# A decoder layer on one core: feed-forward operand sums, hidden loads and the last column blocks in the mixers' pools

## The chip, the core and the metric

The kernel runs on one core of a Trainium2 chip. Times are device microseconds (us) of one execution. The time before is the median of three timed runs; beside it stands one execution taken by the hardware profiler, from which all rows come. PE is TensorE (PEld its weight loads), DVE VectorE, ACT ScalarE, POOL GpSimd, SP SyncE, which here only issues transfers.

## The reference

One layer with 512 tokens (SEQ), D_MODEL 2048 and D_FF 8192, all in float32:

```python
proj = x @ w_in[l]
...
mixed = jax.nn.sigmoid(ga) * y_a + jax.nn.sigmoid(gb) * y_b
x = layer_norm(ALPHA * x + mixed @ w_out[l], ln1_gain[l], ln1_bias[l])
h = jnp.square(jax.nn.relu(x @ w_ff1[l])) @ w_ff2[l]
x = layer_norm(ALPHA * x + h, ln2_gain[l], ln2_bias[l])
```

The change lies in the last two lines and in what joins them to the lines ahead: the two feed-forward products and the second layer norm.

## The kernel before

**Split products.** Every float32 operand is split in two: ACT copies it to a rounded high part, DVE subtracts that from the source for the low part (`split`, L85 and L86). A product is three matmuls, high by high, high by low, low by high (`mm3`, L115 to L117). A raw weight tile of 128 x 1024 thus costs a load of 512 KB, one ACT and one DVE operation, and feeds 24 matmuls of 512 columns, or 24 of 256.

**Up to the feed-forward.** The two mixers, the gated merge and the output projection run first. The output projection's last 256 columns go token tile by token tile: after each, `ln1(t)` normalizes the tile's 128 tokens, transposes them on PE (L646), splits them into the resident operand pair `bh`, `bl` (16 blocks of 128 features x 512 tokens each) and stores the tile to DRAM (`zd`) for the second residual.

**First product, the heads.** It has 32 groups of 256 hidden columns. The first four (NHEAD) are plain products of four raw weight tiles each (`head`); groups 0 and 1 are begun on the first half of the tokens. A group ends with Relu and Square on ACT (L715, L716) and a POOL transfer to DRAM (`keep`, `hd[g]`, L689). Raw tiles and their splits rotate through the mixers' pool `pw` (raw 3, high 3, low 2 buffers).

**First product, Strassen.** Groups 4 to 31 use seven products instead of eight on 256-token halves (`prod1`, q1 to q7). For these, DVE first forms sums of the halves of x from `bh` and `bl` (`whole` and `tt`, L744) and `put` splits them: q6, q7, q3 into tiles of their own, q5 back into the half of `bh`, `bl` that the heads have read. That happens twice (`u`), each time for four of the eight blocks. Weight sums (`b11`, `t2_`, `b12`) are made by DVE per group, results are put together by ACT and DVE (`E`, `U2`, `U3`, `R`), and each group's last two products run inside the next (`tail`, `left`).

**Where the pools change.** All pools of the mixers are closed by `mctx.close()` after the heads; the pools `fw` (raw 7, high 4, low 4) and `fx` of the Strassen part are opened on that memory. A tile in reused memory waits until the last reader of what lay there is done, and the `keep` transfers are such readers. The same happens after the Strassen part, where `fx` is closed and `fy` opened on its place for the hidden operand.

**Second product.** Four blocks of 512 columns (`cg`), each over 32 steps (`k2`) of 256 hidden features. A step loads h from `hd` (again for each block), loads a tile of `w2`, splits both and issues 24 matmuls into four PSUM banks, six for each token tile; the residual tiles come from `zd` on the ACT queue (`resid`, L837), all 16 of them as soon as their memory is free. `close` adds the residual and takes statistics. In the last block the last four steps (RES) are kept: their operands are split into `bh`, `bl`, and each token tile gets its last 24 matmuls, then `close`, layer norm and four output transfers (L894).

**What sets the order.** The program is written as above, and a scheduler then fixes each engine's order and the waits between engines; each engine takes its instructions strictly in that order, the issues of transfers on the ACT and POOL queues among them.

Of the kernel before, what the change touches and what calls it, by code (L numbers as in the profile page):

```python
# [36 lines left out]
RES = 8  # L37
# [15 lines left out]
def layer(ctx, tc, xt, xn, win, wa, wb, wo1, wo2, w1, w2, cst, vec, lnv, out):  # L53
# [533 lines left out]
    pf = mctx.enter_context(tc.tile_pool(name="pf", bufs=1))  # L587
# [95 lines left out]
    def load1(pool, g, b, bufs):  # L683
        raw = pool.tile([P, 1024], F32, tag="raw", bufs=bufs, name=nm("raw"))
        nc.sync.dma_start(out=raw[:], in_=w1[g, b])
        return raw[:]

# [13 lines left out]

    og = {}
# [6 lines left out]
    for g in range(NHEAD):  # L709
        if g not in og:  # L710
            og[g] = [ps("mm"), ps("mm")]
            head(g, og[g], None)
        r = pf.tile([P, 2, T], F32, tag="r", bufs=2, name=nm("r"))
# [25 lines left out]
    for q in ("q6", "q7", "q3"):  # L739
        t_ = fx.tile([P, 2, 8, CG], F32R, tag="x" + q, bufs=1, name=nm("x" + q))  # L740
        xo[q] = (t_[:, 0], t_[:, 1])

    def tt(dst, a, b, op):
        DVE.tensor_tensor(dst, a, b, op=op)  # L744

    for u in range(2):
        k = slice(4 * u, 4 * u + 4)

        def whole(q):
            pool, tag, bufs = (fw, "t2", 2) if q == "q4" else (fx, "st", 3)  # L750
            r = pool.tile([P, 4, CG], F32, tag=tag, bufs=bufs, name=nm("xr"))
            tt(r[:], xo[q][0][:, k, :].bitcast(F32), xo[q][1][:, k, :].bitcast(F32), ALU.add)
            return r

        def put(q, src):
            split(xo[q][0][:, k, :], xo[q][1][:, k, :], src[:])

        a11, a21 = whole("q1"), whole("q5")
        s3 = fw.tile([P, 4, CG], F32, tag="t2", bufs=2, name=nm("s3"))
        tt(s3[:], a11[:], a21[:], ALU.subtract)  # L760
        put("q7", s3)
        a22 = whole("q4")
        tt(a22[:], a21[:], a22[:], ALU.add)
        tt(a11[:], a22[:], a11[:], ALU.subtract)
        put("q6", a11)
        a12 = whole("q2")
        tt(a12[:], a12[:], a11[:], ALU.subtract)
        put("q3", a12)
        put("q5", a22)

    def tmp(tag, bufs):
        return fx.tile([P, CG], F32, tag=tag, bufs=bufs, name=nm(tag))[:]
# [20 lines left out]
    for g in range(NHEAD, NG):  # L793
        A, B, C = ps6(0), ps6(1), ps6(2)
        R = fx.tile([P, 2, T], F32, tag="st", bufs=3, name=nm("R"))
        E, U2, U3 = tmp("E", 2), tmp("U2", 2), tmp("U3", 1)
        b11 = load1(fw, g, 0, 7)
        prod1(A, "q1", b11, True, False)
        ACT.activation(E, A[:, :CG], AF.Copy)
        b12, b22 = load1(fw, g, 1, 7), load1(fw, g, 3, 7)  # L800
        tt(b11, b12, b11, ALU.subtract)
        t2_ = fw.tile([P, 1024], F32, tag="t2", bufs=2, name=nm("t2"))[:]
# [6 lines left out]
        b21 = load1(fw, g, 2, 7)  # L809
# [15 lines left out]
    def hload(k2):
        raw = fw.tile([P, 1024], F32, tag="raw", bufs=7, name=nm("hraw"))
        nc.sync.dma_start(out=raw[:], in_=hd[k2][:])
        return raw[:]

    def w2load(cg, k2):  # L830
        raw = fw.tile([P, 1024], F32, tag="raw", bufs=7, name=nm("raw"))
        nc.sync.dma_start(out=raw[:], in_=w2[cg, k2])
        return raw[:]

    def resid(t, cg):
        z = fy.tile([P, T], F32, tag=f"z{t}_{cg}", bufs=1, name=nm("z"))[:]
        nc.scalar.dma_start(out=z, in_=zd[t][:, cg * T:(cg + 1) * T])  # L837
        zt[t, cg] = z
# [6 lines left out]
    for cg in range(4):  # L845
        end = cg == 3
        o = [ps8() for _ in range(NT)]
        n2 = NG - (RES // 2 if end else 0)
        for k2 in range(n2):
            hh = fy.tile([P, 1024], F32R, tag="hh", bufs=3, name=nm("hh"))  # L850
            hl = fy.tile([P, 1024], F32R, tag="hl", bufs=3, name=nm("hl"))
            split(hh[:], hl[:], hload(k2))
            hh, hl = wview((hh, hl), T)
            wh, wl = wview(wsplit(w2load(cg, k2)), T)
            for k in range(2):
                for t in range(NT):
                    ts = slice(t * P, (t + 1) * P)
                    mm3(o[t][:], hh[:, k, ts], hl[:, k, ts], wh[:, k, :], wl[:, k, :],
                        k2 == 0 and k == 0, not end and k2 == NG - 1 and k == 1)
# [35 lines left out]
    wctx.close()  # L895
# [69 lines left out]
```

## Time and profile before

| | us |
|---|---|
| median of three runs (2744.82 to 2748.64) | 2748.24 |
| profiled execution | 2750.08 |
| its span from first to last instruction | 2748.3 |
| PE busy in it | 2673.1 |
| DVE busy | 1513.8 |
| ACT busy | 1124.3 |

The profiled execution lies 1.84 us over the median; 1.8 us of its time lie outside the span. The busy times say which engine leads. Where that engine stands still is read from its waits and from windows around them. In a window's row, "busy (x)" is the busy time and the number of instructions, and PEclk the granted clock as a share of full speed; two levels occur, 2.4 GHz (1.00) and 1.2 GHz (0.50), and a value between them is a stretch with both.

### The profile page before, as it was taken

What the parts mean: (1) busy time and instruction counts of PE and PEld (TensorE: products, weight loads), DVE (VectorE), ACT (ScalarE), POOL (GpSimd) and SP (SyncE); (2) the same over time, 40 slices, a digit from 0 to 9 for tenths busy, and PEclk for the clock granted to TensorE, in tenths of its full rate; (3) what the DMA queues carried; (4) which work ended last, traced back from release to release, by engine and by line L of the source; (5) the groups of instructions that cost most, each with busy time, mean ns of one, the idle gap of its engine ahead of it and who ended that gap; (6) DMA issues with size and microseconds to landing.
All of it is one profiled execution on the core that took longest, in us unless ns stands there. A gap on an engine that the chain in (4) does not pass through costs nothing. (4 is left out here: it accounts for less than half of the span.)

```text
span 2748.3 us, 37420 instructions
## 1 busy us (share of the span) xinstructions
PE 2673.1 (97%) x15264; PEld 2351.2 (86%) x15264; DVE 1513.8 (55%) x1985; ACT 1124.3 (41%) x1539; POOL 178.9 (7%) x152
## 2 busy tenths in 40 slices
PE   8999999999999999999978999999989999999997
PEld 8889788888888888889968999999978888888885
DVE  4588876564222222434738777777744444544546
ACT  4576646443222222322524454444543333333333
POOL 0110312210000000000200000000000000000001
PEclk9999999999999999999998999999999999999998
DMA  5322222222333333533533444434476566665663
GB/s 183 92 75 72 75 68 79 77 78 85 100 100 93 99 98 94 192 96 119 169 123 100 138 131 126 136 124 138 131 257 196 191 198 192 192 197 190 195 194 113
DMA packets 101549, 364.55 MB, mean 133 GB/s; under 512 B 11392, under 2 KB 12160, under 8 KB 99840
## 3 DMA queue, kind: packets, MB, share of 16 engines
q1 hardware_dynamic: 91584, 326.50, 38.4%
q0 software_dynamic: 5760, 25.17, 2.3%
q10 hardware_dynamic: 4032, 10.49, 1.0%
q8 instruction: 120, 1.97, 0.3%
q14 instruction: 53, 0.43, 0.0%
HBM read 336.94 MB, written 25.17 MB: 132 GB/s over the span
## 5 line engine op out<-in xcount | busy, mean ns | idle before, releaser
L86 DVE TENSOR_TENSOR wl<-raw,wh 128x1024 fp32r<-128x1024 f32 (+1 forms) x503 | 618.7, 1230 | 590.4 <-PE mm L117 335.8
L85 ACT ACTIVATE wh<-raw 128x1024 fp32r<-128x1024 f32 (+1 forms) x503 | 528.1, 1051 | 792.5 <-PE mm L116 585.6
L115 PE MATMUL mm<-bh,wh 128*128 128x512 f32 (+1 forms) x1920 | 665.8, 347 | 10.8 <-ACT wh L85 10.2
L117 PE MATMUL mm<-bh,wl 128*128 128x512 f32 (+1 forms) x1920 | 664.7, 347 | 2.9 <-DVE wl L86 2.9
L116 PE MATMUL mm<-bl,wh 128*128 128x512 f32 (+1 forms) x1920 | 665.9, 347 | 0.0
L115 PEld LDWEIGHTS mm<-bh,wh 128*128 128x128 f32 x1920 | 365.7, 191 | 54.6 <-ACT wh L85 10.9
L117 PEld LDWEIGHTS mm<-bh,wl 128*128 128x128 f32 x1920 | 365.2, 190 | 46.6 <-DVE wl L86 3.6
L116 PEld LDWEIGHTS mm<-bl,wh 128*128 128x128 f32 x1920 | 365.7, 190 | 42.7
L86 DVE TENSOR_TENSOR hl<-hraw,hh 128x1024 fp32r<-128x1024 f32 x124 | 151.7, 1225 | 358.5 <-ACT hh L85 358.5
L85 ACT ACTIVATE hh<-hraw 128x1024 fp32r<-128x1024 f32 x124 | 131.3, 1060 | 413.2 <-PE mm L116 392.6
L115 PE MATMUL mm<-wh,hh 128*128 128x512 f32 x496 | 193.5, 390 | 0.0
L117 PE MATMUL mm<-wh,hl 128*128 128x512 f32 x496 | 193.4, 390 | 0.0
L116 PE MATMUL mm<-wl,hh 128*128 128x512 f32 x496 | 193.4, 390 | 0.0
L115 PE MATMUL mm<-wh,bh 128*128 128x256 f32 (+1 forms) x448 | 139.3, 313 | 6.5 <-ACT bh L85 5.6
L115 PE MATMUL mm<-xq,wh 128*128 128x256 f32 x448 | 127.6, 285 | 16.3 <-ACT wh L85 16.3
L115 PE MATMUL tp<-wh,hh 128*128 128x512 f32 x368 | 143.4, 390 | 0.0
L117 PE MATMUL tp<-wh,hl 128*128 128x512 f32 x368 | 143.4, 390 | 0.0
L116 PE MATMUL tp<-wl,hh 128*128 128x512 f32 x368 | 143.4, 390 | 0.0
L116 PE MATMUL mm<-wl,bh 128*128 128x256 f32 (+1 forms) x448 | 138.7, 311 | 0.8 <-DVE wl L86 0.8
L117 PE MATMUL mm<-wh,bl 128*128 128x256 f32 (+1 forms) x448 | 138.1, 310 | 0.0
L116 PE MATMUL mm<-xq,wh 128*128 128x256 f32 x448 | 127.3, 284 | 0.0
L117 PE MATMUL mm<-xq,wl 128*128 128x256 f32 x448 | 127.3, 284 | 0.0
(295 smaller groups left out, 4496.0 us busy)
## 6 DMA issues: line engine op xcount, KB each, us to landing
raw<-w SPq DMA_DIRECT2D x264, 512.0 KB, 4.2
raw<-win SPq DMA_DIRECT2D x151, 512.0 KB, 3.6
hraw<-hd SPq DMA_DIRECT2D x128, 512.0 KB, 3.3
raw<-wo SPq DMA_DIRECT2D x32, 512.0 KB, 3.6
hd<-R POOLq DMA_DIRECT2D x28, 512.0 KB, 2.9
raw<-wb SPq DMA_DIRECT2D x16, 512.0 KB, 3.6
raw<-wa SPq DMA_DIRECT2D x16, 512.0 KB, 3.5
z<-xn ACTq DMA_DIRECT2D x4, 1024.0 KB, 7.3
```

Of the source, the lines that this page charges most:

```text
L85: ACT.activation(hi, src, AF.Copy)
L86: DVE.tensor_tensor(lo, src, hi.bitcast(F32), op=ALU.subtract)
L115: PE.matmul(o, ah, bh_, start=first, stop=False, skip_group_check=True)
L116: PE.matmul(o, ah, bl_, start=False, stop=False, skip_group_check=True)
L117: PE.matmul(o, al, bh_, start=False, stop=last, skip_group_check=True)
```

## The change

The diff is given without blank lines and without lines that only rename.

- **Pools.** The pools `pm` and `pw` of the mixers stay open to the end. Raw tiles of the feed-forward come two to a tile in `pm`'s four large buffers (`pair`), and `wsplit` deals the split tiles in turn to `pw`'s eight buffers, still four pairs deep.
- **Operand sums.** They get fixed room in one buffer of `pf` that the heads do not use (`room`), and q6, q7 and q3 the other three. `t2_` alternates between two slices of `room`. Results have two buffers instead of three.
- **Second product.** For the first two steps h goes through `wsplit` instead of the pool `fy`. Blocks 0 and 1 run as before. Blocks 2 and 3 run together in all eight PSUM banks: h is loaded and split once for both (48 matmuls a step), so 96 h tiles are loaded instead of 128. The last four steps are kept as before, now 16 blocks of `w2` in `bh`, `bl` and h in its own four buffers; each token tile gets 48 matmuls, two `close`, layer norm and output. The residuals of blocks 2 and 3 come in four loads of 512 KB instead of eight of 256 KB, late in the program.

```diff
-RES = 8
+RES = 4
...
+    pd = ctx.enter_context(tc.tile_pool(name="pd", bufs=1, space=bass.MemoryType.DRAM))
     pa = ctx.enter_context(tc.tile_pool(name="pa", bufs=1))
+    pm = ctx.enter_context(tc.tile_pool(name="pm", bufs=1))
+    pw = ctx.enter_context(tc.tile_pool(name="pw", bufs=1))
     pp = ctx.enter_context(tc.tile_pool(name="pp", bufs=4, space=bass.MemoryType.PSUM))
-    pd = ctx.enter_context(tc.tile_pool(name="pd", bufs=1, space=bass.MemoryType.DRAM))
-    mctx = ExitStack()
-    pm = mctx.enter_context(tc.tile_pool(name="pm", bufs=1))
-    pw = mctx.enter_context(tc.tile_pool(name="pw", bufs=1))
...
-    mctx.close()
...
-    wctx = ExitStack()
-    fw = wctx.enter_context(tc.tile_pool(name="fw", bufs=1))
-    fctx = ExitStack()
-    fx = fctx.enter_context(tc.tile_pool(name="fx", bufs=1))
+    count = [0]
     def wsplit(src):
-        wh = fw.tile([P, 1024], F32R, tag="wh", bufs=4, name=nm("wh"))
-        wl = fw.tile([P, 1024], F32R, tag="wl", bufs=4, name=nm("wl"))
+        i = count[0] % 4
+        count[0] += 1
+        h, l = ("wh", "wh", "wh", "raw")[i], ("wl", "wl", "raw", "raw")[i]
+        room = {"raw": 3, "wh": 3, "wl": 2}
+        wh = pw.tile([P, 1024], F32R, tag=h, bufs=room[h], name=nm("wh"))
+        wl = pw.tile([P, 1024], F32R, tag=l, bufs=room[l], name=nm("wl"))
         split(wh[:], wl[:], src)
         return wh, wl
+    def pair():
+        return pm.tile([P, 2, 1024], F32, tag="mz", bufs=4, name=nm("raws"))
+    def load(dst, src):
+        nc.sync.dma_start(out=dst, in_=src)
+        return dst
...
+    room = pf.tile([P, 4, 1024], F32, tag="h", bufs=4, name="room")
     for q in ("q6", "q7", "q3"):
-        t_ = fx.tile([P, 2, 8, CG], F32R, tag="x" + q, bufs=1, name=nm("x" + q))
+        t_ = pf.tile([P, 2, 8, CG], F32R, tag="h", bufs=4, name=nm("x" + q))
         xo[q] = (t_[:, 0], t_[:, 1])
...
+        whole(r0, "q1")
+        whole(r1, "q5")
+        tt(r2, r0, r1, ALU.subtract)
+        put("q7", r2)
...
+        w = pair()
+        b11, b12 = load(w[:, 0, :], w1[g, 0]), load(w[:, 1, :], w1[g, 1])
...
+        t2_ = room[:, g % 2, :]
...
+        for k2 in range(NG):
+            raw = pair()
+            h = load(raw[:, 0, :], hd[k2][:])
+            w = load(raw[:, 1, :], w2[cg, k2])
+            if cg == 0 and k2 < 2:
+                h = wsplit(h)
+            else:
+                h = hsplit(h)
+            step(o, h, wsplit(w), k2 == 0, k2 == NG - 1)
...
+    os_ = [[ps8() for _ in range(NT)] for _ in range(2)]
+    kept = []
+    for k2 in range(NG):
+        if k2 % 2 == 0:
+            raw = pair()
+        h = hsplit(load(raw[:, k2 % 2, :], hd[k2][:]))
+        ws = pair()
+        ws = [load(ws[:, i, :], w2[2 + i, k2]) for i in range(2)]
+        if k2 < NG - RES:
+            for i in range(2):
+                step(os_[i], h, wsplit(ws[i]), k2 == 0, False)
+        else:
+            kept.append(wview(h, T))
+            for i in range(2):
+                k = i * 2 * RES + 2 * (k2 - NG + RES)
+                split(bh[:, k:k + 2, :].rearrange("p k c -> p (k c)"),
+                      bl[:, k:k + 2, :].rearrange("p k c -> p (k c)"), ws[i])
     gb2 = lnload(1, fy, 1)
-    rh, rl = bh[:, RES:2 * RES, :], bl[:, RES:2 * RES, :]
-    for i in range(RES // 2):
-        ks = slice(2 * i, 2 * i + 2)
-        split(bh[:, ks, :].rearrange("p k c -> p (k c)"), bl[:, ks, :].rearrange("p k c -> p (k c)"),
-              w2load(3, n2 + i))
-        split(rh[:, ks, :].rearrange("p k c -> p (k c)"), rl[:, ks, :].rearrange("p k c -> p (k c)"),
-              hload(n2 + i))
+    for t in range(NT):
+        z = pair()
+        nc.scalar.dma_start(out=z[:, 0, :], in_=zd[t][:, 2 * T:4 * T])
+        for i in range(2):
+            zt[t, 2 + i] = z[:, 0, i * T:(i + 1) * T]
     for t in range(NT):
         ts = slice(t * P, (t + 1) * P)
-        for k in range(RES):
-            mm3(o[t][:], rh[:, k, ts], rl[:, k, ts], bh[:, k, :], bl[:, k, :], False, k == RES - 1)
-        close(t, 3, o[t])
+        for i in range(2):
+            for k in range(2 * RES):
+                hh, hl = kept[k // 2]
+                mm3(os_[i][t][:], hh[:, k % 2, ts], hl[:, k % 2, ts], bh[:, i * 2 * RES + k, :],
+                    bl[:, i * 2 * RES + k, :], False, k == 2 * RES - 1)
+            close(t, 2 + i, os_[i][t])
```

What the change moves is seen in the engines' orders. A row is the line, the operation, out<-in and the size; numbers behind a name tell one tile from another.

**DVE where the heads end.** The last weight tile of the heads is raw_11198, that of the first Strassen product q1 (`b11`) raw_11294 before and raws_11276 now; xr, s and room hold the operand sums. Before:

```order
L86 TENSOR_TENSOR wl_11170<-raw_11168,wh_11169 128x1024
L86 TENSOR_TENSOR wl_11200<-raw_11198,wh_11199 128x1024
L744 TENSOR_TENSOR xr_11245<-bh,bl 128x1024
L744 TENSOR_TENSOR xr_11247<-bh,bl 128x1024
L744 TENSOR_TENSOR xr_11259<-bh,bl 128x1024
L744 TENSOR_TENSOR s_1551_11249<-xr_11245,xr_11247 128x1024
L744 TENSOR_TENSOR xr_11253<-bh,bl 128x1024
L86 TENSOR_TENSOR wl_11297<-raw_11294,wh_11296 128x1024
```

Now:

```order
L85 TENSOR_TENSOR wl_11140<-raw_11138,wh_11139 128x1024
L85 TENSOR_TENSOR wl_11170<-raw_11168,wh_11169 128x1024
L85 TENSOR_TENSOR bl<-room,bh 128x4x256
L751 TENSOR_TENSOR room<-bh,bl 128x1024
L85 TENSOR_TENSOR wl_11200<-raw_11198,wh_11199 128x1024
L751 TENSOR_TENSOR room<-room 128x1024 x2
L751 TENSOR_TENSOR room<-bh,bl 128x1024
L85 TENSOR_TENSOR bl<-room,bh 128x4x256
L85 TENSOR_TENSOR wl_11280<-raws_11276,wh_11279 128x1024
```

Before, all 24 operations of the two rounds stand behind the split of raw_11198. Now 17 of them stand ahead of it, among the heads' splits, and seven behind it.

**ACT at the same place.** E copies the result of q1 (mm), and the room in the row behind it is the weight sum for q6. Before:

```order
L716 ACTIVATE r_11228<-r_11228 128x1024
L85 ACTIVATE wh_11296<-raw_11294 128x1024
L85 ACTIVATE xq_1547_11243<-s_1551_11249 128x1024
L85 ACTIVATE bh<-xr_11253 128x4x256
L799 ACTIVATE E_11291<-mm_11287 128x256
L85 ACTIVATE xq_1546_11242<-xr_11245 128x1024
```

Now:

```order
L84 ACTIVATE bh<-room 128x4x256
L84 ACTIVATE wh_11279<-raws_11276 128x1024
L84 ACTIVATE bh<-room 128x4x256
L84 ACTIVATE xq_1546_11234<-room 128x1024
L713 ACTIVATE r_11228<-mm_11106 128x512
L84 ACTIVATE xq_1548_11236<-room 128x1024
L713 ACTIVATE r_11228<-mm_11107 128x512
L714 ACTIVATE r_11228<-r_11228 128x1024
L802 ACTIVATE E_11273<-mm_11269 128x256
L84 ACTIVATE wh_11313<-room 128x1024
```

Before, E is followed by the splits of the operand sums. Now those stand ahead of it, and the weight split for q6 follows E at once.

**ACT where the Strassen part ends.** R (before) and r (now) are the last group's results; hh is the high part of h, wh of w2. Before:

```order
L789 ACTIVATE R_17331<-R_17331 128x1024
L85 ACTIVATE hh_17623<-hraw_17625 128x1024
L85 ACTIVATE hh_17659<-hraw_17661 128x1024
L85 ACTIVATE hh_17695<-hraw_17697 128x1024
L837 DMA z_18775<-zd_9803 128x512
...
L837 DMA z_22153<-zd_9806 128x512
L85 ACTIVATE hh_17731<-hraw_17733 128x1024
L85 ACTIVATE wh_17775<-raw_17773 128x1024
```

Now:

```order
L791 ACTIVATE r_17232<-r_17232 128x1024
L84 ACTIVATE wh_17598<-raws_17591 128x1024
L84 ACTIVATE wh_17633<-raws_17626 128x1024
L84 ACTIVATE hh_17594<-raws_17591 128x1024
...
L84 ACTIVATE hh_17699<-raws_17696 128x1024
L861 DMA z_18641<-zd_9803 128x512
...
L861 DMA z_19781<-zd_9803 128x512
L84 ACTIVATE wh_17668<-raws_17661 128x1024
L861 DMA z_19785<-zd_9804 128x512
L861 DMA z_19789<-zd_9805 128x512
L861 DMA z_19793<-zd_9806 128x512
L84 ACTIVATE wh_17703<-raws_17696 128x1024
```

Before, the first step's hh stands first behind the last Square, and 16 residual loads stand between the third hh and the fourth. Now the first hh on `fy` is that of the third step (raws_17591), and eight loads stand there, with the split of the fifth step's w2 (raws_17661) among them.

## Rows read from the trace of the kernel before

**Rows 1.** Page, busy time of the engines, and PE in 40 slices (tenths)

```profile
PE 2673.1 (97%) x15264; PEld 2351.2 (86%) x15264; DVE 1513.8 (55%) x1985; ACT 1124.3 (41%) x1539; POOL 178.9 (7%) x152
PE   8999999999999999999978999999989999999997
```

**Rows 2.** PE's waits: us in total, times, longest us

```profile
PE mm L115 <- ACT wh L85: 27.4, 4, 16.3
PE sc L115 <- ACT hh L85: 8.5, 2, 8.3
```

**Rows 3.** Windows: length, busy of PE, PEld, DVE, ACT, POOL, PEclk, DMA share, GB/s

```profile
1326.00:1340.00 14.00, 10.72 (x67) 10.11 (x66) 14.00 (x16) 8.36 (x13) 7.95 (x5) 0.77 0.44 144
1431.00:1437.00 6.00, 4.79 (x24) 4.50 (x24) 6.00 (x6) 1.89 (x2) 0.00 (x0) 0.58 0.97 395
1454.00:1460.00 6.00, 5.70 (x25) 5.12 (x24) 6.00 (x6) 4.17 (x5) 0.00 (x0) 0.50 0.16 26
1480.00:2012.00 532.00, 532.00 (x4435) 532.00 (x4435) 395.26 (x420) 261.64 (x292) 14.36 (x27) 1.00 0.42 132
2028.00:2040.00 12.00, 12.00 (x42) 9.68 (x43) 3.40 (x3) 1.77 (x2) 0.45 (x1) 0.77 0.96 360
2040.00:2050.00 10.00, 9.28 (x40) 7.05 (x39) 2.71 (x3) 3.80 (x4) 0.00 (x0) 1.00 1.01 362
2050.00:2706.00 656.00, 656.00 (x2896) 543.35 (x2895) 305.21 (x271) 246.09 (x246) 0.00 (x0) 1.00 0.60 194
```

**Rows 4.** Timeline where the heads end: start, us, operation, [idle before <-releaser]

```profile
1425.99 3.50 DVE L744 TENSOR_TENSOR xr<-bh,bl 128x1024 f32<-128x1024 f32 x3 [14.31 <-DMA hd<-r]
...
1430.94 0.58 PE L115 MATMUL mm<-bh,wh 128*128 128x256 f32 x1 [10.06 <-ACT wh L85]
...
1432.94 0.58 PE L117 MATMUL mm<-bh,wl 128*128 128x256 f32 x1 [1.21 <-DVE wl L86]
...
1437.25 0.38 ACT L799 ACTIVATE E<-mm 128x256 f32<-128x256 f32 x1 [1.00 <-PE mm L117]
...
1452.38 1.06 ACT L85 ACTIVATE wh<-t 128x1024 fp32r<-128x1024 f32 x1
...
1453.49 0.58 PE L115 MATMUL mm<-xq,wh 128*128 128x256 f32 x1 [16.27 <-ACT wh L85]
```

**Rows 5.** Timeline where the Strassen part ends, same columns

```profile
2026.82 1.06 ACT L85 ACTIVATE hh<-hraw 128x1024 fp32r<-128x1024 f32 x1 [4.21 <-DMA hd<-R]
...
2027.93 0.79 PE L115 MATMUL sc<-wh,hh 128*128 128x512 f32 x1 [8.33 <-ACT hh L85]
...
2046.20 1.06 ACT L85 ACTIVATE hh<-hraw 128x1024 fp32r<-128x1024 f32 x1 [16.43 <-DMA z<-zd]
```

**Rows 6.** Timeline of the end, same columns

```profile
2712.17 0.69 DVE L842 SCALAR_TENSOR_TENSOR z<-z,tp 128x512 f32<-128x512 f32 x1 [14.95 <-PE tp L117]
...
2713.62 0.26 DVE L622 BATCH_NORM_AGGREGATE mv<-stats 128x2 f32<-128x24 f32 x1
...
2720.13 0.68 DVE L842 SCALAR_TENSOR_TENSOR z<-z,mm 128x512 f32<-128x512 f32 x1
...
2720.72 0.74 DVE L893 SCALAR_TENSOR_TENSOR z<-z,mv,gb 128x512 f32<-128x512 f32 x1
...
2728.06 0.39 PE L117 MATMUL mm<-bh,bl 128*128 128x512 f32 x1
...
2741.33 3.08 DVE L893 SCALAR_TENSOR_TENSOR z<-z,mv,gb 128x512 f32<-128x512 f32 x3
```

**Rows 7.** Timeline where the last token tiles are normalized, same columns

```profile
1319.70 0.68 DVE L637 TENSOR_TENSOR z<-z,gb 128x512 f32<-128x512 f32 x1
...
1330.57 1.76 DVE L637 TENSOR_TENSOR z<-z,gb 128x512 f32<-128x512 f32 x1
...
1332.47 0.63 PE L646 MATMUL tp<-ident,z 128*128 128x128 f32 x4 [1.60 <-DVE z L637]
1334.60 0.58 PE L117 MATMUL mm<-bh,wl 128*128 128x256 f32 x1 [1.49 <-DVE wl L86]
```

More of the change, by code (lines that the diff above doesn't have):

```diff
@@ L584, in layer @@
     pr_ctx.close()
-    pf = mctx.enter_context(tc.tile_pool(name="pf", bufs=1))
+    fctx = ExitStack()
+    pf = fctx.enter_context(tc.tile_pool(name="pf", bufs=1))
     zs = []
@@ L680, in layer @@
         ln1(t)
[L683 to L686, printed above, removed]
     def keep(g, r):
@@ L700, in head, with result @@
                         part != 1 and kc == 0, part != 0 and kc == KC - 1)
+    def result():
+        return pf.tile([P, 2, T], F32, tag="r", bufs=2, name=nm("r"))
     og = {}
@@ L712, in layer @@
             head(g, og[g], None)
-        r = pf.tile([P, 2, T], F32, tag="r", bufs=2, name=nm("r"))
+        r = result()
         for m in range(2):
@@ L747, in layer, with whole @@
         k = slice(4 * u, 4 * u + 4)
[L749 to L753, printed above, removed]
-        def put(q, src):
[L756 to L769, printed above, removed]
+        r0, r1, r2, r3 = (room[:, i, :].rearrange("p (k c) -> p k c", k=4) for i in range(4))
+        def whole(r, q):
+            tt(r, xo[q][0][:, k, :].bitcast(F32), xo[q][1][:, k, :].bitcast(F32), ALU.add)
+        def put(q, src):
+            split(xo[q][0][:, k, :], xo[q][1][:, k, :], src)
+        whole(r0, "q1")
+        whole(r1, "q5")
+        tt(r2, r0, r1, ALU.subtract)
+        put("q7", r2)
+        whole(r3, "q4")
+        tt(r3, r1, r3, ALU.add)
+        tt(r0, r3, r0, ALU.subtract)
+        put("q6", r0)
+        whole(r1, "q2")
+        tt(r1, r1, r0, ALU.subtract)
+        put("q3", r1)
+        put("q5", r3)
     def tmp(tag, bufs):
-        return fx.tile([P, CG], F32, tag=tag, bufs=bufs, name=nm(tag))[:]
+        return pf.tile([P, CG], F32, tag=tag, bufs=bufs, name=nm(tag))[:]
     def prod1(o, q, src, first, last):
@@ L778, in prod1 @@
                 first and k == 0, last and k == 7)
-    def ps6(i):
-        return ps(("mm", "mm", "tp")[i])
     def tail(g, B, C, U2, U3, E, t4, b22, R):
@@ L793, in layer @@
     for g in range(NHEAD, NG):
-        A, B, C = ps6(0), ps6(1), ps6(2)
-        R = fx.tile([P, 2, T], F32, tag="st", bufs=3, name=nm("R"))
+        A, B, C = ps("mm"), ps("mm"), ps("tp")
+        R = result()
         E, U2, U3 = tmp("E", 2), tmp("U2", 2), tmp("U3", 1)
-        b11 = load1(fw, g, 0, 7)
+        w = pair()
+        b11, b12 = load(w[:, 0, :], w1[g, 0]), load(w[:, 1, :], w1[g, 1])
         prod1(A, "q1", b11, True, False)
         ACT.activation(E, A[:, :CG], AF.Copy)
-        b12, b22 = load1(fw, g, 1, 7), load1(fw, g, 3, 7)
+        w = pair()
+        b22, b21 = load(w[:, 0, :], w1[g, 3]), load(w[:, 1, :], w1[g, 2])
         tt(b11, b12, b11, ALU.subtract)
-        t2_ = fw.tile([P, 1024], F32, tag="t2", bufs=2, name=nm("t2"))[:]
+        t2_ = room[:, g % 2, :]
         tt(t2_, b22, b11, ALU.subtract)
@@ L808, in layer @@
         prod1(C, "q5", b11, True, False)
-        b21 = load1(fw, g, 2, 7)
         prod1(A, "q2", b21, False, True)
@@ L819, in layer, with hsplit @@
     fctx.close()
-    fy = wctx.enter_context(tc.tile_pool(name="fy", bufs=1))
+    fy = ctx.enter_context(tc.tile_pool(name="fy", bufs=1))
     zt = {}
[L825 to L838, printed above, removed]
+    def hsplit(src):
+        hh = fy.tile([P, 1024], F32R, tag="hh", bufs=4, name=nm("hh"))
+        hl = fy.tile([P, 1024], F32R, tag="hl", bufs=4, name=nm("hl"))
+        split(hh[:], hl[:], src)
+        return hh, hl
     def close(t, cg, o):
@@ L843, in close @@
         DVE.bn_stats(stats[:, t, cg, :], zc)
-    for cg in range(4):
-        end = cg == 3
-        o = [ps8() for _ in range(NT)]
[L848 to L859, printed above, removed]
-        for t in range(NT):
-            resid(t, cg)
-            if not end:
-                close(t, cg, o[t])
@@ L865, in layer, with step @@
-    gb2 = lnload(1, fy, 1)
-    rh, rl = bh[:, RES:2 * RES, :], bl[:, RES:2 * RES, :]
-    for i in range(RES // 2):
-        ks = slice(2 * i, 2 * i + 2)
-        split(bh[:, ks, :].rearrange("p k c -> p (k c)"), bl[:, ks, :].rearrange("p k c -> p (k c)"),
-              w2load(3, n2 + i))
-        split(rh[:, ks, :].rearrange("p k c -> p (k c)"), rl[:, ks, :].rearrange("p k c -> p (k c)"),
-              hload(n2 + i))
+    def step(o, h, w, first, last):
+        hh, hl = wview(h, T)
+        wh, wl = wview(w, T)
+        for k in range(2):
+            for t in range(NT):
+                ts = slice(t * P, (t + 1) * P)
+                mm3(o[t][:], hh[:, k, ts], hl[:, k, ts], wh[:, k, :], wl[:, k, :], first and k == 0, last and k == 1)
@@ new lines, in layer @@
+    for cg in range(2):
+        o = [ps8() for _ in range(NT)]
+        for k2 in range(NG):
[7 more added lines that the diff above has]
+            step(o, h, wsplit(w), k2 == 0, k2 == NG - 1)
+        for t in range(NT):
+            z = fy.tile([P, T], F32, tag=f"z{t}_{cg}", bufs=1, name=nm("z"))
+            nc.scalar.dma_start(out=z[:], in_=zd[t][:, cg * T:(cg + 1) * T])
+            zt[t, cg] = z[:]
+            close(t, cg, o[t])
@@ L873, in layer @@
+    gb2 = lnload(1, fy, 1)
+    for t in range(NT):
+        z = pair()
+        nc.scalar.dma_start(out=z[:, 0, :], in_=zd[t][:, 2 * T:4 * T])
+        for i in range(2):
+            zt[t, 2 + i] = z[:, 0, i * T:(i + 1) * T]
     for t in range(NT):
         ts = slice(t * P, (t + 1) * P)
-        for k in range(RES):
-            mm3(o[t][:], rh[:, k, ts], rl[:, k, ts], bh[:, k, :], bl[:, k, :], False, k == RES - 1)
-        close(t, 3, o[t])
+        for i in range(2):
[4 more added lines that the diff above has]
+            close(t, 2 + i, os_[i][t])
@@ L894, in layer @@
             (nc.sync if c % 2 else nc.scalar).dma_start(out=out[t * P:(t + 1) * P, c * T:(c + 1) * T], in_=zcs[c])
-    wctx.close()
 def _constants():
```

## Prediction

> **What bounds the kernel now.** I read the busy times first: PE is busy 2673.1 of 2748.3 us [rows 1], so almost all that a change of order can win lies where PE stands still or runs slowly. The slices show where: PE falls below nine tenths in the first, in the 20th to 22nd, in the 30th and in the last [rows 1]. PE's own waits name two of these places. It waits 27.4 us in four stretches for high parts of weights and 8.5 us for high parts of h [rows 2]. The windows add what the waits don't count, matmuls at the lower granted clock, and they give the full pace: 532.00 us for 4435 matmuls of 256 columns, 0.120 us each, and 656.00 us for 2896 of 512 columns, 0.2265 us each, with PE busy all the time in both [rows 3]. In these two stretches, 1188 us long, PE is the bound; DVE is at 395 of 532 and 305 of 656 us there. The change leaves the matmuls as they are, so it can win only at the seams.
>
> **Seam 1, heads to Strassen: what is removed.** The first Strassen matmul comes after an idle 10.06 us; ahead of it DVE stood 14.31 us and was released by the transfer of the heads' last result (DMA hd<-r) [rows 4]. That is the pools' wait: the sums' tiles lie on memory that this transfer reads. Then DVE works through the sums: PE waits 1.21 us in q1 and 16.27 us behind it, until ACT has split the first weight sum at 1452.38 [rows 4]. Together 27.54 us. Around these waits the clock falls: 24 matmuls take 4.79 us at 0.58 where 2.88 would do, and 25 take 5.70 us at 0.50 where 3.00 would do [rows 3], so 1.91 + 2.70 us more. The seam costs 32.2 us.
>
> **Seam 1: what is left.** The sums no longer wait for that transfer, and 17 of the 24 operations stand among the heads' splits. I count from T, when PE starts the second half of the last head, two tiles of 24 matmuls or 10.9 us before the heads' end. DVE takes 1.14 us from one sum's start to the next (three in 3.50 us, overlapping a little [rows 4]). Its remaining work from the split of q5 to the weight sum for q6 is 13 operations, 14.8 us. It can begin 1.6 us before T: half a tile's matmuls (2.7 us) before T the last head has passed the first four blocks, and ACT's part takes 1.06. So the sum is there at T + 13.2, while q1 ends at T + 10.9 + 24 x 0.120 = T + 13.8: DVE is just in time. ACT is not. Its order has E, which needs the end of q1, ahead of the split of that sum. E takes 0.38 us and began about 0.2 us after q1's end [rows 4], the split 1.06, so PE waits some 1.6 us, and some 1.0 more for the two splits behind, which come at ACT's and DVE's pace. I take 2.6 us. Bounds: 0, if the scheduler's order of matmuls covers it, and 6, if DVE is three operations later; beyond that 2.7 us if the clock falls again, the price of the second such stretch [rows 3]. **Gain 32.2 - 2.6 = 29.6 us, bounds 23.5 and 32.2.**
>
> **The heads, which pay for it.** One sum (1.14 us) now stands early in the third `ln1`, in a stretch where DVE is busy 14.00 of 14.00 us and PE 10.72 [rows 3]; PE waits there for DVE, 1.60 us for z and 1.49 for a weight's low part [rows 7]. In a stretch that DVE sets, an operation more costs its length: 1.1 us. The other sums come later, between weight splits due every 2.9 us, with two low buffers; where three stand together (3.4 us) a split may be late by about 1 us. The order of splits and z operations changes too, and can win back part of the 3.1 us of waits. **I take -1.2 us, bounds -6 and +4.** The same rows show an L637 of 0.68 us taking 1.76 while POOL works (POOL is busy 7.95 of 14.00 there) [rows 3, 7]. The Trainium skill, "SBUF — State Buffer", section "Who interferes with whom", says why: a DVE operation with two SBUF inputs and a GpSimd one that reads SBUF exclude each other for a whole instruction. By that rule, with which the row agrees, the early sum may be held as well, for 1.76 - 0.68 = 1.1 us more: -2.3 us in place of -1.2, and a result of 2703 in place of 2702.
>
> **Strassen groups.** Each of the 28 takes 168 x 0.120 = 20.2 us. Rotation, pairs and two result buffers instead of three change what a load or a split waits for, not what PE does. ACT is busy 262 and DVE 395 of 532 us, and DMA 0.42 [rows 3]; a tile that is free half a group earlier or later costs nothing under that cover. **0 us**; if the cover were gone, the slower rival below.
>
> **Seam 2, Strassen to the second product.** Here PE idles 8.33 us: the first hh sits on `fy`, so ACT waited for the last group's transfer (DMA hd<-R) till 2026.82 [rows 5]. After it 42 matmuls take 12.00 us where 9.51 would do, a loss of 2.49, and 40 take the 10.00 us in which 9.06 would do, 0.94, as ACT's splits stand behind 16 residual loads for 16.43 us [rows 3, 5]. In all 11.8 us. Now two steps of 24 x 0.2265 = 5.4 us need nothing from `fy`, so PE has 10.9 us of cover. The transfer lands 7.2 us after the last Strassen matmul (2026.82 against 2027.93 - 8.33 = 2019.60 [rows 5]); with two w2 splits ahead of it in ACT's order, hh (1.06 us) is ready at about 8.7. Next late are the fifth and sixth steps, whose w2 splits stand among eight residual loads. They are due 21.8 and 27.2 us after the seam, and the loads carry half the bytes of before; DMA, at 0.96 and 1.01 here [rows 3], can still make them late. I take 1 us, bounds 0 and 3.5. **Gain 10.8 us, bounds 8.3 and 11.8.**
>
> **Blocks 2 and 3 together.** A third less h splits; PE's stretch is unaffected: a step has three DVE splits, 3.4 us, beside 48 matmuls, 10.9 us. **0 us**, up to 1 lost where eight banks change hands.
>
> **The end.** The last matmul starts at 2728.06 and takes 0.39; the span ends at 2748.3, so 19.85 us follow. DVE is the cause: it was still closing the third and fourth tile, since a tile's 24 matmuls take 5.4 us and its chain more: from the statistics at 2713.62 to the end of the last L893 at 2721.46, less the 0.59 of another tile's close, 7.25 us, with 1.45 for the close ahead of it (2712.17 to 2713.62) [rows 6]. Now a tile has 48 matmuls, 10.9 us, and DVE 1.45 + 1.45 + 7.25 = 10.15 us: it keeps up. After the last matmul come one close, one chain and the output, from the last L893's end at 2744.41 to 2748.3 [rows 6], 3.9: 1.45 + 7.25 + 3.9 = 12.6 us. **Gain 7.25 us, bounds 6 and 8.5.**
>
> **Sum.** 29.6 - 1.2 + 10.8 + 7.25 = 46.4 us. The profiled execution took 2750.08 us, giving 2703.7; the median is 1.84 lower, giving 2701.8.
>
> **Rivals.**
> - *Seam 1 only half closed.* DVE, delayed in the heads, makes the sum for q6 late, and the clock falls there: 3.4 + 2.7 us, and 4.8 in the heads, 10.9 in all: 2713. For it: DVE has 0.6 us to spare at q6. Against: by the count E, not DVE, comes last there.
> - *The change doesn't do at seam 2 what it says.* If h of the first steps still waits for the transfer, 8.33 of the 10.8 us stay, and the clock's 2.49: 2713. Against: the order has no hh of `fy` ahead of the third step.
> - *A wait in every Strassen group, slower.* A `pair` is free only when both halves have been used, so a load can start up to a group later, and a split waits for it. Over 28 groups the gain is gone from 46.4 / 28 = 1.66 us a group; at 2 us the kernel takes 2758. Against it stands PE without a pause and the idle half of DMA and ACT [rows 3].
> - *All seams close and the heads gain*: 2692.
>
> **How the numbers follow.** Forecast, 2695 to 2709: 0.65. Seam 1 half closed: 0.16. Seam 2 unchanged: 0.06. Heads gain: 0.09. A wait per group: 0.04, nearly all of it slower. The range 2692 to 2714 takes in the bounds of the terms that don't all fall one way. Within 0.2% (5.5 us), about what a measurement tells from no change, needs a wait of just 1.5 to 1.8 us a group: 0.01.
>
> **What would show it.** PE's waits for wh fall from 27.4 to under 7 us and that for hh disappears; no DVE wait on hd<-r stays; after q1 a PE wait of 1 to 2 us ends with ACT's split of the room's sum; from the last matmul to the end it is 12 to 13 us. Wrong would be: windows in the Strassen stretch with PE under 99%, a clock below 1.00 at the second seam, or a stretch of the heads more than 5 us longer.

## The result, and the profile after

The changed kernel takes 2698.48 us (median of four runs, 2697.32 to 2703.13) against 2747.74 for the kernel before (also of four): ratio 0.9826, interval 0.9809 to 0.9843. Forecast were 2702 us, in a range from 2692 to 2714. Measured a second time, beside the kernel before on one chip, it took 2699.71 against 2748.49: 0.9820, 0.9807 to 0.9834. The profiled execution took 2697.93 us, 52.15 less than that of before (2750.08).

The page of the changed kernel, busy times and PE in 40 slices; the dips of [rows 1] in the 21st, 22nd and 30th slice are gone (the 20th, which the prediction names too, was full):

```profile
PE 2662.0 (99%) x15264; PEld 2341.7 (87%) x15264; DVE 1479.9 (55%) x1953; ACT 1094.4 (41%) x1507; POOL 177.2 (7%) x152
PE   8999999999999999999999999999999999999998
```

PE's waits in it (us in total, times, longest). Against [rows 2], 27.4 us for wh have become 3.5, and the wait for hh is no longer in the list; DVE's wait for hd<-r (14.31 us [rows 4]) is gone too:

```profile
PE mm L114 <- ACT wh L84: 3.5, 4, 1.4
...
PE mm L116 <- DVE wl L85: 1.6, 3, 0.6
```

Windows of it, columns as in [rows 3]: the last token tiles, the first seam, the Strassen stretch, the second seam (two rows), and what follows the last matmul:

```profile
1326.00:1340.00 14.00, 11.64 (x95) 11.03 (x94) 14.00 (x18) 10.49 (x15) 6.80 (x5) 1.00 0.65 235
...
1420.00:1430.00 10.00, 8.14 (x65) 7.71 (x64) 9.56 (x10) 6.19 (x7) 0.53 (x1) 1.00 0.23 77
...
1460.00:1980.00 520.00, 520.00 (x4335) 519.95 (x4333) 385.57 (x409) 253.97 (x284) 13.82 (x26) 1.00 0.39 133
...
1984.00:2000.00 16.00, 16.00 (x82) 13.62 (x82) 8.24 (x9) 9.70 (x10) 1.59 (x3) 1.00 0.60 185
2000.00:2020.00 20.00, 20.00 (x90) 16.56 (x89) 9.83 (x9) 7.85 (x9) 0.00 (x0) 1.00 1.02 403
...
2683.10:2696.10 13.00, 0.01 (x1) 0.00 (x0) 8.49 (x16) 2.76 (x5) 2.55 (x2) 0.60 0.24 88
```

PE is at work through the whole second seam, at the full clock, where it idled 8.33 us [rows 5]. In the Strassen stretch PE still has no pause. Both kernels issue the same number of matmuls, so the starts of the n-th matmul in two traces can be subtracted, and the difference shows in which stretch it grows:

| stretch (us more than the changed kernel) | before | before, again | changed, again |
|---|---|---|---|
| first 20 us of the program | 1.55 | 2.36 | 1.40 |
| output projection's end and heads | 0.55 | -1.36 | -0.98 |
| first seam | 30.75 | 31.27 | 1.48 |
| Strassen groups | 0.00 | 0.00 | 0.00 |
| second seam | 12.49 | 12.35 | -0.02 |
| second product | 0.00 | 0.00 | 0.00 |
| behind the last matmul | 6.90 | 7.16 | 0.01 |

The first line is one program's own spread: the two traces of the changed kernel differ there by 1.40 us. It is no part of the change.

At the first seam the timeline of the changed kernel shows the chain that the prediction had counted out (start, us, operation, [idle before <-releaser]):

```profile
1420.47 1.22 DVE L751 TENSOR_TENSOR room<-raws,raws 128x1024 f32<-128x1024 f32 x1
...
1421.90 0.38 ACT L802 ACTIVATE E<-mm 128x256 f32<-128x256 f32 x1 [0.94 <-PE mm L116]
1422.18 1.05 ACT L84 ACTIVATE wh<-room 128x1024 fp32r<-128x1024 f32 x1
...
1423.28 0.39 PE L114 MATMUL mm<-xq,wh 128*128 128x256 f32 x1 [1.42 <-ACT wh L84]
...
1424.22 0.39 PE L114 MATMUL tp<-bh,wh 128*128 128x256 f32 x1 [0.44 <-ACT wh L84]
```

DVE's weight sum ends at 1421.69, ACT is at E until 1422.2, and PE waits 1.42 us and then 0.44, where [rows 4] had 10.06, 1.21 and 16.27.

### The profile page after: what moved, and what is told of

It reads as the page before. It is cut to its first block, busy times and chain, and to the rows that moved or that the text cites. A ratio compares the mean times of both kernels' runs of the same rounds, so it can differ in the third digit from the quotient of the medians.

```text
span 2696.1 us, 37095 instructions
## 1 busy us (share of the span) xinstructions
PE 2662.0 (99%) x15264; PEld 2341.7 (87%) x15264; DVE 1479.9 (55%) x1953; ACT 1094.4 (41%) x1507; POOL 177.2 (7%) x152
## 4 chain that ended last, share of the span: by engine, by line
PE 94%; DVE 4%; ACT 1%; DMA 1%; issue 0%; POOL 0%; SPq 0%; DVEq 0%; ACTq 0%
PE mm L116 23%; PE mm L115 23%; PE mm L114 23%; PE tp L114 6%; PE tp L116 6%; PE tp L115 6%; PE sc L116 1%; PE sc L114 1%; PE sc L115 1%; PE tp L444 1%; DVE wl L85 1%; PE tp L285 0%; PE tp L277 0%; DMA raw<-w 0%; DMA raw<-win 0%
## 5 line engine op out<-in xcount | busy, mean ns | idle before, releaser
L85 DVE TENSOR_TENSOR wl<-raw,wh 128x1024 fp32r<-128x1024 f32 (+1 forms) x239 | 295.4, 1236 | 490.8 <-PE mm L116 311.5
L84 ACT ACTIVATE wh<-raw 128x1024 fp32r<-128x1024 f32 (+1 forms) x239 | 250.4, 1048 | 549.9 <-PE mm L115 393.1
L85 DVE TENSOR_TENSOR wl<-raws,wh 128x1024 fp32r<-128x1024 f32 x262 | 320.1, 1223 | 224.7 <-ACT wh L84 224.5
L84 ACT ACTIVATE wh<-raws 128x1024 fp32r<-128x1024 f32 x262 | 276.2, 1055 | 393.6 <-PE mm L115 241.8
L85 DVE TENSOR_TENSOR hl<-raws,hh 128x1024 fp32r<-128x1024 f32 x94 | 114.8, 1224 | 228.5 <-ACT hh L84 228.4
L84 ACT ACTIVATE hh<-raws 128x1024 fp32r<-128x1024 f32 x94 | 99.1, 1058 | 260.2 <-PE mm L115 255.0
L114 PE MATMUL mm<-wh,hh 128*128 128x512 f32 x472 | 183.6, 389 | 0.0
L115 PE MATMUL mm<-wl,hh 128*128 128x512 f32 x472 | 183.6, 389 | 0.0
L116 PE MATMUL mm<-wh,hl 128*128 128x512 f32 x472 | 183.6, 389 | 0.0
L114 PE MATMUL mm<-xq,wh 128*128 128x256 f32 x448 | 126.9, 283 | 1.4 <-ACT wh L84 1.4
```

Source lines behind the costliest of these rows:

```text
L114: PE.matmul(o, ah, bh_, start=first, stop=False, skip_group_check=True)
L115: PE.matmul(o, ah, bl_, start=False, stop=False, skip_group_check=True)
L116: PE.matmul(o, al, bh_, start=False, stop=last, skip_group_check=True)
```

## The experiments

The theory: each seam cost what the pools' wait held up, and the end cost DVE's backlog. Each part is undone alone in the first three runs. Up to "Three parts together" each is one execution, profiled. Edits are to the changed kernel unless the text says otherwise, and "us more" is against its trace, by the table's stretches.

**The sums late again.**

```diff
+    fctx.close()
+    fctx = ExitStack()
+    pf = fctx.enter_context(tc.tile_pool(name="pf2", bufs=1))
     room = pf.tile([P, 4, 1024], F32, tag="h", bufs=4, name="room")
```

> The changed kernel, but the pool of the operand sums is closed and opened anew where the heads end, so that every sum waits for the heads' last transfer to DRAM. Theory (the first seam cost what the pools' wait and the 24 sums behind it cost): DVE's first sum starts about 5 us after the last head matmul, behind DMA hd<-r; q1 runs meanwhile, as its weights need no sum; the product q6 starts 26 to 29 us after the last head matmul where it now starts 4.2 us after it; the clock falls to 0.5 once more (2 to 4 us): in all 24 to 29 us longer, some 2722 to 2728 us. The heads lose the sums' company and gain up to 3 us back. Rival (the gain comes from the open weight pools, the sums' place matters little): under 10 us longer.

Measured: 2729.96 us, 31.22 us more at the first seam and nothing behind it; the heads, without the sums, were 0.5 us faster, where up to 3 had been expected. The rows of its timeline, DVE's first sum, ACT's split for q6 and PE's product:

```profile
1424.69 3.50 DVE L754 TENSOR_TENSOR room<-bh,bl 128x1024 f32<-128x1024 f32 x3 [6.72 <-DMA hd<-r]
...
1452.59 1.06 ACT L84 ACTIVATE wh<-room 128x1024 fp32r<-128x1024 f32 x1 [0.20 <-DVE room L754]
...
1453.75 0.55 PE L114 MATMUL mm<-xq,wh 128*128 128x256 f32 x1 [31.30 <-ACT wh L84]
```

The same releaser as in [rows 4], and 27.9 us from the first sum to the split where it was 26.4. The weight pools stay open here, and q1 did run at once, but that gains nothing: its 2.9 us are only waited for later. The whole gain of the seam is the sums' earlier start. How much of it is the wait of 6.72 us and how much the sums' place behind it, this run doesn't separate. The expectation was 2 us short at its upper end for the time, and 5 us for q6: it put q6 26 to 29 us behind the heads, and q6 came after q1's 2.9 us and 31.30 of waiting, some 34 us.

**The first two h on the late pool.**

```diff
-            if cg == 0 and k2 < 2:
-                h = wsplit(h)
-            else:
-                h = hsplit(h)
+            h = hsplit(h)
```

> The changed kernel, but h of the second product's first two steps goes through the pool opened behind the Strassen part, like all later steps. Theory (the second seam was a pool waiting for the last group's transfer): PE waits 8 to 9 us for ACT's hh behind DMA hd<-r, and the matmuls behind it lose 2.5 us at the lower clock: 10 to 12 us longer, some 2708 to 2710. The part of the old loss that came from 16 residual loads (0.9 us) does not come back, since only 8 stand there. Rival (loads of w2 and h are late there too, and the open pools matter): under 5 or over 15 us longer.

Measured: 2708.00 us, 9.12 us more at the second seam (and 1.49 at the first, of which below). ACT's and PE's rows:

```profile
1994.13 1.06 ACT L84 ACTIVATE hh<-raws 128x1024 fp32r<-128x1024 f32 x1 [3.35 <-DMA hd<-r]
...
1995.28 0.77 PE L114 MATMUL sc<-wh,hh 128*128 128x512 f32 x1 [7.51 <-ACT hh L84]
```

The wait is the one of [rows 5], and two tiles' detour through `wsplit` removes it. The 9.12 us are less than the 10 to 12 expected: the wait was to be 8 to 9 us and is 7.51, the clock was to cost 2.5 and costs 1.5. The kernel before lost 12.4 us here. 9.12 is what its pool cost. Of the other 3.4 us in its first trace, 1.3 lie where its 16 residual loads held up ACT (a fourth hh 16.43 us late [rows 5]), and the rest in a longer wait (8.33 against 7.51) and a longer stretch at the lower clock; in its second trace 2.6 of 3.2 us lie at the residual loads.

**Blocks 2 and 3 apart.** Block 3 alone has kept steps, so that a tile ends with 24 matmuls and one close:

```diff
-    for cg in range(2):
+    for cg in range(3):
...
-        for i in range(2):
-            for k in range(2 * RES):
...
-            close(t, 2 + i, os_[i][t])
+        for k in range(2 * RES):
...
+        close(t, 3, o3[t])
```

> The changed kernel, but column blocks 2 and 3 run one after the other; the last four steps of block 3 alone are kept, so a token tile ends with 24 matmuls, one close and its layer norm. Theory (the end is DVE's backlog: 8.7 us of chain per tile against 5.4 us of matmuls): 18.5 to 20 us from the last matmul to the end where it is 13.0 now: 6 to 7 us longer, some 2704 to 2706, and nothing changes ahead of the kept steps, although a third more h is loaded and split. Rival (the end gains by the later and larger residual loads or by fewer splits): under 3 us longer.

Measured: 2708.42 us. From the last matmul to the end 20.77 us instead of 12.96, 7.81 more, a little over the 18.5 to 20 expected; nothing changed between the seam and the last matmul, though h was split 32 times more.

**Two kept steps instead of four** (`RES = 2`), 24 matmuls and two closes a tile.

> The changed kernel, but two steps are kept instead of four: a token tile ends with 24 matmuls, two closes and its layer norm, 10.15 us of DVE's work against 5.4 us of matmuls. Theory (backlog): DVE falls behind by 4.7 us at each of three tiles, 14 us less what it is ahead at the first: 22 to 27 us from the last matmul to the end, 9 to 14 us longer, some 2708 to 2712. Rival (the last tile's chain alone counts, whatever the tiles before do): 13 us from the last matmul to the end, no longer than now.

Measured: 2704.61 us; 21.50 us from the last matmul to the end, 8.54 more, where 22 to 27 us were expected. The windows behind the last matmul, of blocks apart and of two kept steps, beside the 13.00 us with DVE busy 8.49 of the changed kernel:

```profile
2685.88:2706.65 20.77, 0.00 (x0) 0.00 (x0) 17.02 (x31) 5.68 (x10) 8.59 (x5) 0.58 0.41 152
```

```profile
2681.25:2702.70 21.45, 0.00 (x0) 0.00 (x0) 17.71 (x32) 5.87 (x11) 7.76 (x5) 0.56 0.40 147
```

In both, DVE has 31 or 32 instructions left where the changed kernel has 16: the backlog is there, and the last tile's chain alone doesn't set the end. The size was overrated: the chain of 10.15 us a tile is not all work. In the run with two kept steps DVE is busy 35.25 us for all four tiles, 8.8 a tile, since while it is behind it fills the gaps of one tile's chain with the next tile's operations.

**E on DVE.** Of the 1.42 us that are left at the first seam:

```diff
-        ACT.activation(E, A[:, :CG], AF.Copy)
+        if g > NHEAD:
+            ACT.activation(E, A[:, :CG], AF.Copy)
+        else:
+            DVE.tensor_scalar(E, A[:, :CG], 1.0, None, op0=ALU.mult)
```

> The changed kernel, but in the first Strassen group DVE copies q1's result (E) instead of ACT, so that ACT's split of the weight sum for q6 stands behind nothing that waits for q1. Theory of the prediction's step (E on ACT sets PE's wait behind q1, DVE's sum is there 0.2 to 0.6 us earlier): the split starts when the sum ends, about 0.45 us earlier, and PE's wait of 1.42 us falls to 0.9 to 1.1. Rival (DVE sets it, E costs nothing): 1.3 to 1.5 us as now. Either way the time moves by under 1 us.

Measured: 2700.15 us, no less in the total; ACT's split and PE's row in its timeline:

```profile
1424.23 1.06 ACT L84 ACTIVATE wh<-room 128x1024 fp32r<-128x1024 f32 x1 [0.75 <-DVE room L751]
...
1425.34 0.39 PE L114 MATMUL mm<-xq,wh 128*128 128x256 f32 x1 [0.96 <-ACT wh L84]
```

0.96 instead of 1.42, as expected: E on ACT cost 0.46 us, and DVE's sum, which now releases ACT's split, sets the rest.

**The heads' weights.** In the changed kernel PE waited in the heads where the kernel before did not. SP's queue and ACT there:

```profile
1343.84 2.02 SPq L92 DMA_DIRECT2D raw<-w  x2
1350.19 0.96 SPq L740 DMA_DIRECT2D raws<-w  x2
...
1352.07 1.06 ACT L84 ACTIVATE wh<-raw 128x1024 fp32r<-128x1024 f32 x1 [5.49 <-DMA raw<-w]
```

The pair issued at 1350.19 reuses the last token tile's buffer and had to wait for its store; heads' weights stand behind it, and the idea was that ACT waited for these. So this pair went to POOL's queue:

```diff
+        q = nc.gpsimd if g == NHEAD + 1 else nc.sync
-        b22, b21 = load(w[:, 0, :], w1[g, 3]), load(w[:, 1, :], w1[g, 2])
+        b22, b21 = load(w[:, 0, :], w1[g, 3], q), load(w[:, 1, :], w1[g, 2], q)
```

> The changed kernel, but the fourth pair of Strassen weights, whose buffer held the last token tile until its store to DRAM (zd) has landed, is loaded from the POOL queue, where it stands behind that store anyway, and no longer from SP's queue ahead of the heads' next weights. Theory (SP's queue stood still for that landing and made ACT wait 5.49 us for a head's weights, PE 0.67 and 0.79): these waits go, and from the 7060th to the 7240th matmul PE is 1.5 to 3.2 us faster. Rival (the weights are late because transfers fill the DMA engines, 313 GB/s in that stretch, or because the sums hold DVE): under 0.5 us faster.

Measured: 2701.33 us, and 2.0 us slower in the heads, not faster. PE waits at the same place, 1.07 and 0.60 us. SP's queue is not the cause, and the rows above already say so: the two loads that ACT waited for had been issued at 1343.84 and 1345.53, ahead of the pair. They took 8.1 and 7.7 us to land, 8.5 and 7.9 in this run, where the kernel before has 5.0 and 4.3 at the same place. Then the second group's two pairs were held back until the second head had its result:

```diff
+            late = pl.tile([P, 1], F32, name="late")
+            DVE.tensor_scalar(late[:], r[:, 0, 0:1], 1.0, None, op0=ALU.mult)
...
         w = pair()
+        if g == NHEAD + 1:
+            DVE.tensor_scalar(w[:, 0, 0:1], late[:], 1.0, None, op0=ALU.mult)
+            DVE.tensor_scalar(w[:, 1, 0:1], late[:], 1.0, None, op0=ALU.mult)
```

> The changed kernel, but the second Strassen group's two weight pairs (2 MB) are loaded only when the second head's result is there: DVE writes one column of their tiles from it first. That takes these 2 MB out of the stretch in which the last token tiles' stores and the heads' weights share the DMA engines, some 80 us before the pairs are used. Theory (the heads' weights are late because transfers fill the DMA engines): PE's waits of 0.67 and 0.79 us for wh at the 7128th and 7130th matmul and of 0.53 for wl at the 7180th go, and from the 7060th to the 7240th matmul PE is 1.5 to 3 us faster than in the changed kernel. Rival (the sums among the heads' splits hold DVE, or the buffers are late): under 0.5 us faster, with the waits still there.

Measured: 2700.95 us. The waits at the 7128th and 7130th matmul are gone, 1.47 us faster from the 7060th to the 7240th, just under the 1.5 expected, and the two loads land after 4.7 and 4.3 us. The DMA engines are busy 0.95 of the time from 1342 to 1352 us in the changed kernel, 0.76 here. So late landings beside other transfers are the likely cause of these waits; they vary from one execution to the next: the run with two kept steps, of the same order up to there, has landings of 5.8 and 6.5 us and neither wait. But 0.6 us came up ahead of that stretch and 0.4 behind it, and the heads as a whole are 0.52 us faster. Among seven executions of kernels that are alike up to the heads' end the heads as a whole spread from -1.42 to +1.00, so it isn't shown that the time gains by it. ACT still waits 11.8 us for raw<-w between 1326 and 1366 us, 11.2 in the changed kernel; that three raw buffers are too few is a candidate that was not tried.

**The last tile without POOL.**

```diff
-            (POOL if c == 3 else DVE).tensor_tensor(zcs[c], zcs[c], gs[c], op=ALU.mult)
-        ACT.activation(zcs[3], zcs[3], AF.Copy, scale=y)
-        POOL.tensor_tensor(zcs[3], zcs[3], bs[3], op=ALU.add)
+            (POOL if c == 3 and t < NT - 1 else DVE).tensor_tensor(zcs[c], zcs[c], gs[c], op=ALU.mult)
+        if t < NT - 1:
+            ACT.activation(zcs[3], zcs[3], AF.Copy, scale=y)
+            POOL.tensor_tensor(zcs[3], zcs[3], bs[3], op=ALU.add)
...
-            if c < 3:
+            if c < 3 or t == NT - 1:
```

> The changed kernel, but the last token tile's fourth column block is normalized by DVE (two operations) instead of POOL (two) and ACT (one). Theory (a DVE operation with two inputs in SBUF stands still while POOL works: L628 1.25 instead of 0.16 us, L907 1.75 instead of 0.68): those two are short again, 2.2 us, and DVE does two operations of 0.6 and 0.66 us more: 0.7 to 1.2 us less from the last matmul to the end, 12.0 instead of 13.0. Rival (the durations are long for another reason): 1.3 us more, 14.3.

Measured: 2698.09 us; 11.25 us behind the last matmul instead of 12.96, 1.71 less. The small operation, one product and DVE's last operation of the last tile, with POOL's rows in the changed kernel and then without POOL:

```profile
2686.03 1.27 POOL L907 TENSOR_TENSOR raws<-raws,gb 128x512 f32<-128x512 f32 x1 [6.88 <-ACT raws L904]
2686.07 1.25 DVE L628 SCALAR_TENSOR_TENSOR mv<-mv 128x1 f32<-128x1 f32 x1
...
2688.69 1.28 POOL L909 TENSOR_TENSOR raws<-raws,gb 128x512 f32<-128x512 f32 x1 [1.39 <-ACT raws L908]
2688.76 1.75 DVE L907 TENSOR_TENSOR raws<-raws,gb 128x512 f32<-128x512 f32 x1
...
2691.10 0.74 DVE L912 SCALAR_TENSOR_TENSOR raws<-raws,mv,gb 128x512 f32<-128x512 f32 x1
```

```profile
2688.46 0.15 DVE L628 SCALAR_TENSOR_TENSOR mv<-mv 128x1 f32<-128x1 f32 x1
...
2689.20 0.69 DVE L907 TENSOR_TENSOR raws<-raws,gb 128x512 f32<-128x512 f32 x1
...
2691.20 1.41 DVE L913 SCALAR_TENSOR_TENSOR raws<-raws,mv,gb 128x512 f32<-128x512 f32 x2
```

1.10 + 1.06 us are gone from these two rows. From the last matmul's end to the end of DVE's last operation it is 7.64 us where it was 8.73: 1.1 less, within the 0.7 to 1.2 us expected. The other 0.6 us lie behind DVE, 3.6 us to the end where it was 4.2, and had not been expected; the last three output transfers are issued over 1.3 us here and within 0.7 there, which may be why. The Trainium skill's rule from "SBUF — State Buffer", section "Who interferes with whom", that a DVE instruction with two SBUF inputs contends with a GpSimd one that reads SBUF, holds here: L628 stands until POOL's instruction has ended.

**The kernel before, again.**

> The kernel before, once more. It tells what in the comparison of the two traces is the kernel's and what one execution's. If the lower clock while the last token tiles are normalized (0.77 from 1326 to 1340 us) belongs to the kernel's order, it is there again, with about 3.3 us lost against the changed kernel; the two seams' waits of 10.06, 16.27 and 8.33 us are there within 0.3 us; the first 20 us of the program may differ by 1.5 us, as they did among the other runs.

Measured: 2749.61 us; the table above has its stretches. The seams cost 0.5 us more and 0.1 less than in the first trace; PE's wait behind q1 is 15.8 us instead of 16.3, a little beyond what was expected. The lower clock at the last token tiles is not there again. The window of that stretch (14 us, shifted by 1 us) in this execution, against 10.72 busy at 0.77 in [rows 3]:

```profile
1327.00:1341.00 14.00, 10.21 (x81) 9.39 (x80) 14.00 (x14) 10.01 (x14) 7.86 (x5) 1.00 0.44 149
```

**Three parts together, and the changed kernel beside it.** E on DVE, the second group's pairs late and the last tile without POOL.

> The changed kernel with three parts together: E of the first group on DVE, the second group's pairs late, the last token tile without POOL. If the parts add up: 0.45 us at the first seam, 1.5 to 3 in the heads, 1.7 at the end, 3.6 to 5.2 us in all; and the clock, which fell behind the wait of 1.42 us in four executions of seven, is not let down after a wait of 0.96: up to 1.5 us more in such executions. Some 2693 to 2696 us, ratio to the kernel before 0.980 to 0.9815. If they do not add up: no more than 1 us below the changed kernel.

> The changed kernel once more, on the same chip and in the same rounds, to compare with: 2697 to 2701 us, ratio to the kernel before 0.981 to 0.984.

Measured: 2697.20 us (2696.46 to 2701.24), ratio 0.9814, 0.9801 to 0.9827; the changed kernel 2699.71, 0.9820. The medians differ by 2.5 us, less than the 3.6 that the parts would add up to, and the intervals overlap, so the timing doesn't tell the two apart. The traces do at one place: behind the last matmul it is 11.25 against 12.97 us. The clock fell at the first seam here too, after 0.96 us of waiting, which the expectation had excluded, and the heads gained no more than the changed kernel's own second execution (0.87 and 0.98 us).

## Why the prediction was right

**Seam 1 (29.6 us forecast, bounds 23.5 and 32.2): right, 30.75 and 31.27, or 29.3 and 29.8 against the changed kernel's second trace.** The chain held link by link. Counted from T (1408.2, from the heads' end at 1419.1), the sum was forecast at T + 13.2 and ended at T + 13.5; E stood ahead of the split; PE waited 1.42 us where 1.6 were forecast, and 0.44 where 1.0 were. What was left to a bound, the clock, happens: in six of eight executions with this wait it fell (0.87 of full over the 13 us from 1419 us), and the seam was 1.3 to 1.5 us longer; the profiled execution and that with two kept steps are the exceptions. The forecast had priced the fall at 2.7. The gains of 30.75 and 31.27 us are thus those of the rarer case. The same 13 us in the profiled execution and in the changed kernel's second one, columns as in [rows 3]:

```profile
1419.00:1432.00 13.00, 11.14 (x90) 10.68 (x89) 12.49 (x13) 7.16 (x9) 0.53 (x1) 1.00 0.32 118
```

```profile
1419.00:1432.00 13.00, 11.14 (x75) 10.61 (x74) 11.97 (x12) 7.57 (x9) 0.53 (x1) 0.87 0.30 106
```

PE is busy for 11.14 us in both, but with 90 matmuls in the one and 75 in the other.

**Heads (-1.2 us, bounds -6 and +4): within the bounds, the size partly by luck.** The difference to the kernel before is +0.55 in one pair of traces and -1.36 in the other, and executions of the same order spread as far, so the size is not confirmed. The early sum did take its 1.2 us on DVE; POOL did not hold it, and the dearer price of -2.3 did not come up:

```profile
1319.79 1.21 DVE L751 TENSOR_TENSOR room<-bh,bl 128x1024 f32<-128x1024 f32 x1
```

Up to the 7060th matmul the change gained all the same, 1.5 us in one pair and 3.4 in the other, which has the lower clock of one execution in it. The run with the sums late has PE's waits of before there (1.60 and 1.50 us) and not that gain, so it came with the order that the early sums bring. The loss came later, 3.1 us in both pairs, where head weights landed late; the prediction had put loads nowhere in this term. With the sums late that later stretch was 2.2 us shorter, but the heads as a whole just 0.5 us, so what the sums cost in all is no larger than the spread. One row was also read wrongly: 0.77 of the clock in [rows 3] was one execution's, not the kernel's.

**Strassen groups and blocks 2 and 3 together (0 us): right**, 0.00 us in both. The rival of a wait in every group falls with it.

**Seam 2 (10.8 us, bounds 8.3 and 11.8): right in mechanism, 12.4 measured, above its bound.** The step that failed is the term that took 1 us as left: nothing is left, PE has no gap there. And the cost of before was put at 11.8, where matmul by matmul it is 12.4: 1.3 us (2.6 in the second trace) lie at the residual loads, for which the window gave 0.94.

**End (7.25 us): right**, 6.90 and 7.16; 12.96 us are left where 12.6 were forecast. The close of 1.45 us is there and the chain takes 7.24 (7.25 forecast); behind DVE's last operation it is 4.2 where 3.9 were taken. That the cadence of a tile against DVE's chain decides is shown by both experiments on it.

**Sum.** 46.4 us forecast; 49.3 between the medians. The two terms that came out larger are the seams, the second by 1.6 us, the first by 1.2 to 1.7 where the clock doesn't fall and by at most 0.3 either way where it does.

## What to carry to other kernels

Closing a pool is a barrier that no line of the code shows: whatever is opened on its memory waits for the last transfer that reads it, and the work that could have filled the wait then stands behind it. Operand sums placed in free memory cost the same DVE time, but beside matmuls. At the end of a kernel give each output tile more matmul time than its chain takes on the vector engine, and keep the last chain off engines that block each other.

## What the runs showed of the hardware

The same wait of 1.42 us at the same place lowered the granted clock in six executions of eight and not in two, at a price of 1.3 to 1.5 us; a wait of 0.96 us lowered it in one of two; each had one of 0.44 or 0.45 us behind it. At the program's start the granted clock from 6 to 20 us is 0.88 in seven of 13 traces and 1.00 in six, whatever the kernel; the seven are 1.2 to 2.4 us behind the profiled execution of the changed kernel after that stretch, the six between 0.5 ahead and 1.3 behind. And a DVE operation on 128 x 1 elements (L628) took 1.25 us while POOL multiplied, 0.15 without. Loads of 512 KB took 8.1 and 7.7 us to land where the DMA engines were busy 0.95 of the time, 4.7 and 4.3 at 0.76.
